# A 3x3 convolution with 2x2 max pooling on one core: a new program order, one half difference and four head operations on other engines

## The chip, the cores and the metric

The kernel runs on one core of a Trainium2 chip. The metric is the device time of one execution in microseconds (us). The core has five instruction queues, each worked through in order: PE (TensorE, matrix products, with its weight loads shown as PEld), DVE (VectorE), ACT (ScalarE), POOL (GpSimd) and SP (SyncE, which here only issues DMAs). They meet through semaphores alone.

## The reference

```python
x      = randn(16, 64, 64, 64)           # batch, c_in, h, w, float32
weight = randn(128, 64, 3, 3) * 0.1
x_pad  = pad(x, 1 on each side of h and w)
conv[b, co] += weight[co, ci, kh, kw] * x_pad[b, ci, kh:kh+64, kw:kw+64]   # over ci, kh, kw
output[b, c, i, j] = max(conv[b, c, 2*i:2*i+2, 2*j:2*j+2])                 # 16 x 128 x 32 x 32
```

## The kernel before, in words

Two images share the 128 partitions: lane h=0 is the first image of a pair (64 channels on partitions 0 to 63), h=1 the second. Each pair is cut into four bands of eight output rows (R = 8, so sixteen input rows), 32 *steps* s = 0 to 31 in all. For a step and a lane two PSUM banks of 8 x 64 are needed, `ta` and `tb`, out of eight.

The convolution of two neighbouring rows is not computed twice. By a row transform, differences and sums of the input rows meet differences and sums of the weight taps, so that two output rows cost four row products (five in K steps) instead of six. There are two kinds of steps:

- **K steps** (`KSTEPS`, ten) read bf16 rows straight from `kx`, which GpSimd's DMA queue loads with a cast to bf16 (LK, L109 and L114), and need only one sum of rows, KS (L356, VectorE). Their products are PA1, PA2, PB1, PB2 and PR.
- **W steps** (`WSTEPS`, twenty-two) read float32 rows from one of six buffers `wx`, loaded through SyncE (L and LB, L137; a buffer serves two steps). They need three transformed operands: E (`we`, L407: difference of neighbouring rows, GpSimd, or VectorE for the steps in `DIFF_ON_VECTOR`), D (`wd`, L416: difference over two rows, GpSimd, 128 x 1024) and WS (`ws`: sum of neighbouring rows, VectorE). WS has three forms: a two-operand addition (L395), a reduction (L387, steps in `SUM_BY_REDUCTION`), or, for `ODD_ROWS_IN_PSUM`, an addition whose second operand ScalarE has first copied to a PSUM bank (XC, L370, then L374). Their products are P2 (on E), P0 and P3 (on D) and P1 (on WS).

A *product* is three matmuls (L252), one for each column of the 3x3 kernel, on 64 rows of the array. Products of lane 0 and of lane 1 are issued in turn (`product`, L308), one matmul of each, so that both halves of the array work; two such products are called a pair here.

After the products: EV (L468 for K, L470 for W) copies `ta` to SBUF on ScalarE and frees its bank; SE (L481) copies `ta` to `tb` on ScalarE; MX (L498) takes the maximum of `tb` and EV's copy in place on VectorE, and later products (PR or P1), the same for both rows, are added on top; OD (L502) copies the odd columns out on ScalarE; CM (L508) takes the maximum over columns on VectorE and frees the bank of `tb`; ST (L516, L519) stores the step.

The *head* prepares the weights and the first two steps. The nine taps arrive in `wraw`. g0, g1 and g2 cast them to bf16 (L225 or L227); D2 and D0 are differences of taps (L539, L540); GS, GM and GP form sums (L541, L231, L233); u.. repeats a column (L182). T.. transposes a block on TensorE (L198) and V.. copies it to `wt` (L215 to L221). Step 0 has its rows cast in parts: XOa, XOb, XEa, XEb (L524 on ScalarE, L526 on VectorE), and step 2 by X1 and X2 (L533, ScalarE). F.k.part are the half products of step 0, G.k.part those of step 1; Ea and Eb (L428, VectorE) and Da and Db (`wd_half`, L436 to L449) are the half differences of step 1, and SEa, SEb its seeds (L494).

**What sets the order.** Nothing is reordered by a compiler. `ORDER` (L570) is one list of about 750 names; each engine gets its instructions in that order, and a name such as `MX.5.1` stands for step 5, lane 1. The list also decides which PSUM bank is taken (`free`, a queue). Two more waits are put in by hand: an operation of GpSimd made through `on_gpsimd` (L91) waits for the last operation made through `on_vector` (L87), that is the last VectorE operation on SBUF operands alone, reductions not counted; and a load named LB (`late_load`, L459) waits for the same. SyncE's queue holds loads and stores together.

Of the kernel before, what the change touches and what calls it, by code (L numbers as in the profile page):

```python
# [11 lines left out]
def kernel(  # L12
# [27 lines left out]
    SUM_BY_REDUCTION = (1, 3, 11, 12, 19, 20, 24, 25, 31,)  # L40
    ODD_ROWS_IN_PSUM = (4, 6, 8, 14, 17, 22, 23,)
    TURNED_BY_SCALAR = ("D0", "MP",)
    HALVES_ON_VECTOR = ()
    CAST_BY_SCALAR = ("XEa", "XOa", "XOb",)
    TAPS_BY_VECTOR = ()
# [119 lines left out]
    D2, G0, D0, G2, G1, GM, GP = BLOCKS.values()  # L165
# [401 lines left out]
    for m in PRODUCTS:  # L567
# [103 lines left out]
```

## Time and profile before

| | us |
|---|---|
| median of 3 runs | 104.76 (104.11 to 105.74) |
| the profiled execution | 104.74 |
| its span, first to last instruction | 102.9 |

The profiled execution's time exceeds its span by 1.8 us. In the lists of groups and in the timeline a row names the source line, the engine, the operation and its tiles (output <- input), and in brackets what ended the idle time before it. The granted clock of TensorE was full in every slice but the last. The largest loads on SyncE's queue are 480 to 576 KB each, and their median time from issue to landing is 9.0 us; from 2 to 27 us of the span the DMA engines are busy nearly throughout.

The groups of VectorE, ScalarE and GpSimd that carry most of the time besides the matmuls:

| line | what | count | mean ns |
|---|---|---|---|
| L416 POOL | D | 21 | 2361 |
| L407 POOL | E | 17 | 1273 |
| L498 DVE | MX | 64 | 689 |
| L508 DVE | CM | 64 | 414 |
| L387 DVE | WS by reduction | 9 | 1229 |
| L395 DVE | WS by addition | 6 | 764 |
| L470, L468 ACT | EV | 44, 20 | 611, 601 |
| L481 ACT | SE | 42 | 593 |

### The profile page before, as it was taken

Reading aid. Unit: us, or ns where it says so; the run is one execution under the profiler, and the core shown is the slowest. Engines: PE = TensorE matmul, PEld = TensorE weight load, DVE = VectorE, ACT = ScalarE, POOL = GpSimd, SP = SyncE. Lnnn points to the kernel's source line nnn. Section 1 sums busy time; section 2 is a strip of 40 time slices with the busy share of each in tenths; the row PEclk is TensorE's granted clock in tenths of the full one; section 3 lists DMA queues with packets and bytes.
Section 4 is the critical chain, followed back from the end, with each engine's and each line's share of the span. In section 5 each row is a group of like instructions: output and inputs, shape, how many; then the busy total and the mean of one; then the engine's idle time right before and its main releaser. Section 6 shows DMA issues by size and latency. Waiting matters only on the chain.

```text
span 102.9 us, 2528 instructions
## 1 busy us (share of the span) xinstructions
PE 96.5 (94%) x904; PEld 58.8 (57%) x904; DVE 90.0 (87%) x175; ACT 86.0 (84%) x192; POOL 79.8 (77%) x67
## 2 busy tenths in 40 slices
PE   6999999959999999999999999999999999999930
PEld 2475575525564556666666678877866655555400
DVE  1475999959998899999999999998999999799970
ACT  4569797579989799997898989899798899798740
POOL 6172998984995999979996999989599997981000
PEclk9999999999999999999999999999999999999996
DMA  2999999999839999999989868920881621159644
GB/s 68 321 345 305 261 344 344 358 423 314 158 83 295 317 270 362 283 344 411 421 324 130 147 206 197 324 84 0 241 253 47 232 80 38 64 181 322 218 156 151
DMA packets 13789, 24.25 MB, mean 236 GB/s; under 512 B 1104, under 2 KB 9296, under 8 KB 13776
## 3 DMA queue, kind: packets, MB, share of 16 engines
q1 hardware_dynamic: 12528, 21.73, 62.0%
q0 software_dynamic: 1104, 2.23, 13.4%
q8 instruction: 7, 0.11, 0.5%
q10 hardware_dynamic: 144, 0.13, 0.4%
q14 instruction: 6, 0.05, 0.2%
HBM read 17.92 MB, written 8.39 MB: 256 GB/s over the span
## 4 chain that ended last, share of the span: by engine, by line
PE 78%; DMA 10%; DVE 3%; ACT 3%; issue 1%; DVEq 0%; SPq 0%; ACTq 0%
PE acc L252 73%; DMA wx<-in_x_dram 10%; PE acc L628 3%; PE acc L198 2%; DVE o L508 1%; ACT ev L468 1%; ACT kx L533 1%; DVE acc L498 1%; ACT acc L370 1%; DVE ks L356 0%; DVE we L407 0%; DVE we L428 0%; DVEq L666 0%; SPq L137 0%; DVEq L498 0%
## 5 line engine op out<-in xcount | busy, mean ns | idle before, releaser
L252 PEld LDWEIGHTS <-wt 64*128 64x128 bf16 x870 | 55.8, 94 | 35.2 <-issue 3.3
L252 PE MATMUL acc<-wd,wt 64*128 64x504 bf16 (+3 forms) x276 | 53.9, 367 | 0.0
L416 POOL TENSOR_TENSOR wd<-wx 128x1024 bf16<-128x1024 f32 x21 | 49.3, 2361 | 3.3 <-DVE ks L356 3.1
L252 PE MATMUL acc<-kx,wt 64*128 64x504 bf16 (+6 forms) x264 | 45.0, 351 | 0.0
L498 DVE TENSOR_TENSOR acc<-acc,ev 128x512 f32<-128x512 f32 x64 | 42.0, 689 | 1.6 <-PE acc L252 1.1
L252 PE MATMUL acc<-we,wt 64*128 64x512 bf16 (+3 forms) x138 | 31.8, 367 | 1.3 <-ACT ev L468 1.2
L252 PE MATMUL acc<-ws,wt 64*128 64x512 bf16 (+1 forms) x132 | 32.5, 377 | 0.0
L470 ACT ACTIVATE ev<-acc 128x512 f32<-128x512 f32 x44 | 26.2, 611 | 2.1 <-PE acc L252 1.7
L481 ACT COPY acc<-acc 128x512 f32<-128x512 f32 x42 | 24.5, 593 | 1.9 <-PE acc L252 0.9
L508 DVE TENSOR_TENSOR o<-acc,od 128x256 f32<-128x256 f32 x64 | 24.9, 414 | 1.1 <-ACT od L502 0.9
L502 ACT COPY od<-acc 128x256 f32<-128x256 f32 x64 | 23.2, 384 | 2.5 <-PE acc L252 2.0
L407 POOL TENSOR_TENSOR we<-wx 128x512 bf16<-128x512 f32 x17 | 21.4, 1273 | 4.4 <-PE acc L252 3.8
L252 PE MATMUL acc<-ks,wt 64*128 64x504 bf16 (+1 forms) x60 | 13.6, 377 | 0.0
L468 ACT COPY ev<-acc 128x512 f32<-128x512 f32 x20 | 11.8, 601 | 1.9 <-PE acc L252 1.7
L387 DVE TENSOR_REDUCE ws<-wx 128x512 bf16<-128x1024 f32 x9 | 11.1, 1229 | 0.0
L374 DVE TENSOR_TENSOR ws<-wx,acc 128x512 bf16<-128x512 f32 x7 | 4.7, 677 | 1.5 <-ACT acc L370 1.5
L370 ACT COPY acc<-wx 128x512 f32<-128x512 f32 x7 | 4.2, 602 | 1.6 <-DMA wx<-in_x_dram 1.6
L356 DVE TENSOR_TENSOR ks<-kx 128x512 bf16<-128x512 bf16 x10 | 4.4, 449 | 0.6 <-ACT kx L533 0.6
L395 DVE TENSOR_TENSOR ws<-wx 128x512 bf16<-128x512 f32 x6 | 4.5, 764 | 0.0
L628 PE MATMUL acc<-const-bfloat16-1.0 128*128 128x512 bf16 x8 | 3.6, 625 | 0.8 <-PEq L652 0.8
L443 POOL TENSOR_TENSOR wd<-wx 128x512 bf16<-128x512 f32 x2 | 2.5, 1262 | 1.8 <-DVE we L428 1.8
L227 ACT CAST wq<-wraw 128x192 bf16<-128x192 f32 x3 | 1.5, 535 | 1.7 <-DMA wraw<-in_weight_dram 1.7
(33 smaller groups left out, 27.4 us busy)
## 6 DMA issues: line engine op xcount, KB each, us to landing
out_dram<-o SPq DMA_DIRECT2D x27, 256.0 KB, 3.7
wx<-in_x_dram SPq DMA_DIRECT2D x8, 512.0 KB, 9.4
wx<-in_x_dram SPq DMA_DIRECT2D x7, 576.0 KB, 8.3
wx<-in_x_dram SPq DMA_DIRECT2D x3, 544.0 KB, 10.2
kx<-in_x_dram POOLq DMA_DIRECT2D x3, 544.0 KB, 7.8
wx<-in_x_dram SPq DMA_DIRECT2D x3, 480.0 KB, 5.9
out_dram<-o SPq DMA_DIRECT2D x9, 128.0 KB, 4.4
ksecond<-in_x_dram SPq DMA_DIRECT2D x1, 544.0 KB, 5.1
```

The costliest lines, as they stand in the source:

```text
L252: nc.tensor.matmul(acc[t][:, i0:i1, o0:o1], wt[lo : lo + CI, tap_of(m0, kw, h), :], rows(lo, i0, i1, c0, c1), start=start and kw == 1, sto ...
L370: nc.scalar.copy(out=acc[copied[s]], in_=t[:, f + 1 : f + 2 * R : 2, :])
L387: nc.vector.tensor_reduce(out=row["ws", s], in_=t[:, f : f + 2 * R, :].rearrange("p (r two) w -> p r w two", two=2), axis=mybir.AxisListTy ...
L407: inst = (nc.vector if vector else nc.gpsimd).tensor_tensor(out=row["we", s], in0=t[:, f : f + 2 * R : 2, :], in1=t[:, f + 1 : f + 2 * R : ...
L416: nc.gpsimd.tensor_tensor(out=row["wd", s], in0=t[:, f + 1 : f + 1 + 2 * R, :], in1=t[:, f - 1 : f - 1 + 2 * R, :], op=SUB)
L468: nc.scalar.copy(out=ev[s, h], in_=acc[t])
L470: nc.scalar.mul(ev[s, h], acc[t], -1.0)
L481: nc.scalar.copy(out=acc[t], in_=acc[ta[s, h]])
L498: nc.vector.tensor_tensor(out=t, in0=t, in1=ev[s, h], op=MAX)
L502: nc.scalar.copy(out=od[s, h], in_=acc[tb[s, h]][:, :, 1::2])
L508: nc.vector.tensor_tensor(out=ot[s][:, h], in0=acc[t][:, :, 0::2], in1=od[s, h], op=MAX)
L628: nc.tensor.matmul(acc[n].rearrange("p a b -> p (a b)"), ones[:, 0:128], ones, start=True, stop=True, skip_group_check=True)
```

## The change

The list `ORDER` is replaced as a whole; six lists of names change with it. Step kinds, buffers, tiles and all functions stay.

```diff
-    SUM_BY_REDUCTION = (1, 3, 11, 12, 19, 20, 24, 25, 31,)
+    SUM_BY_REDUCTION = (1, 3, 11, 12, 19, 20, 24, 30,)
-    TURNED_BY_SCALAR = ("D0", "MP",)
-    HALVES_ON_VECTOR = ()
-    CAST_BY_SCALAR = ("XEa", "XOa", "XOb",)
-    TAPS_BY_VECTOR = ()
+    TURNED_BY_SCALAR = ("MP",)
+    HALVES_ON_VECTOR = ("Db",)
+    CAST_BY_SCALAR = ("XEa", "XEb", "XOb",)
+    TAPS_BY_VECTOR = ("g1",)
```

So Db goes from GpSimd to VectorE; g1, VD0 (the copy of transposed block D0) and XOa go from ScalarE to VectorE, and XEb from VectorE to ScalarE. Step 25 and step 31 get their sums by addition, step 30 by reduction. The start of the list, up to the place where both orders reach the products of step 4 and step 7:

```diff
-        g2 D2 g0 TD2 D0 TD0 XOa TG0 VD2 F.0.0 GS TG2 g1 XOb VG0 GM F.1.0 uG1 XEb LB.3 VD0 F.0.1 F.1.1 GP VG2 XEa
-        EV.0.1 L.11 X2 X1 LK.0.0 uGM F.2.0 PA1.2.0 KS.0 LB.4 Ea uGP F.3.0 TG1 KS.2 F.2.1 TMP Eb F.3.1 PA1.2.1
-        VMP LB.8 MX.0.1 EV.0.0 G.0.0 PA2.2.1 Da VG1 G.0.1 MX.0.0 SEa.0 SEa.1 Db LB.6 PA2.2.0 WS.1 SEb.1 PR.0.1
-        SEb.0 LK.0.1 E.3 PR.0.0 P2.3.1 PB1.2.1 EV.2.1 G.1.0 G.1.1 PB2.2.1 G.2.0 OD.0.0 G.2.1 EV.2.0 WS.3 EV.1.0
-        EV.1.1 PB1.2.0 PB2.2.0 CM.0.0 OD.0.1 SE.3.1 MX.1.0 CM.0.1 LB.9 D.3 MX.2.0 P2.3.0 P1.1.0 PR.2.0 P0.3.1
-        SE.3.0 P0.3.0 EV.3.1 MX.1.1 P3.3.1 P1.1.1 OD.2.0 MX.2.1 E.11 P3.3.0 MX.3.1 ST.0 PR.2.1 P1.3.1 OD.1.0
-        EV.3.0 PA1.5.0 PA1.5.1 E.4 OD.1.1 CM.2.0 CM.1.0 MX.3.0 CM.1.1 OD.2.1 PA2.5.1 PB1.5.0 P1.3.0 L.14 PB2.5.0
-        D.4 OD.3.1 XC.6 PA2.5.0 E.6 CM.2.1 L.12 P2.4.1 P2.4.0 CM.3.1 XC.4 PA1.7.0 LK.1.0 EV.5.1 PB1.5.1 WS.6
-        PB2.5.1 WS.4 L.16 SE.4.1 OD.3.0 PA2.7.0 P0.4.1 KS.5 P3.4.1 WS.9 KS.7 D.8 EV.5.0 SE.4.0 PA1.7.1 CM.3.0
...
+        g0 g1 g2 D2 XOb TG0 XEb uG1 TD2 TG1 TG2 D0 XOa LB.3 L.11 TD0 VD2 F.0.0 VG0 GS F.1.0 F.0.1 GM XEa VG2
+        F.1.1 EV.0.0 VD0 LB.4 EV.0.1 F.2.0 F.2.1 F.3.1 X1 LK.0.0 uGM KS.0 X2 GP uGP PA1.2.0 LB.6 VG1 F.3.0
+        MX.0.1 LB.8 TMP Ea KS.2 PR.0.1 VMP Eb OD.0.1 G.0.0 G.0.1 MX.0.0 SEa.0 PR.0.0 WS.1 Da Db SEa.1 E.3
+        PA1.2.1 SEb.1 PA2.2.0 LK.0.1 PA2.2.1 SEb.0 PB1.2.0 OD.0.0 G.2.0 CM.0.0 PB2.2.0 EV.2.0 WS.3 G.1.0 G.2.1
+        G.1.1 P2.3.1 EV.2.1 LB.9 L.14 D.3 PB1.2.1 EV.1.0 EV.1.1 SE.3.1 E.11 MX.1.0 PB2.2.1 CM.0.1 P2.3.0 P0.3.1
+        SE.3.0 P1.1.0 P3.3.1 EV.3.1 E.4 ST.0 MX.2.0 PR.2.0 P0.3.0 MX.1.1 P1.1.1 OD.2.0 P3.3.0 OD.1.0 MX.2.1
+        MX.3.1 PA1.5.0 PR.2.1 P1.3.1 CM.1.0 PA2.5.0 OD.1.1 CM.2.0 D.4 EV.3.0 XC.4 CM.1.1 MX.3.0 PB1.5.0 OD.3.1
+        PA1.5.1 WS.4 PA2.5.1 P1.3.0 CM.3.1 KS.5 L.17 EV.5.0 OD.2.1 PB2.5.0 E.6 P2.4.0 P2.4.1 XC.6 CM.2.1 WS.6
+        PB1.5.1 PA1.7.0 OD.3.0 SE.4.1 PB2.5.1 P0.4.1 CM.3.0 PA1.7.1 PA2.7.0 EV.5.1 SE.4.0 L.12 P0.4.0 KS.7 WS.9
...
```

GpSimd's queue in the middle, as the two lists give it (other engines' names left out):

```
before  D.3 E.11 E.4 D.4 E.6 LK.1.0 D.8 D.6 D.9 E.12 D.11 LK.1.1 D.12 E.14 D.14 E.19 E.16 D.16 D.15 E.17 E.20
after   D.3 E.11 E.4 D.4 E.6 LK.1.0 D.6 D.8 D.9 LK.1.1 D.11 D.12 E.12 E.14 D.14 E.19 E.20 E.16 D.15 D.16 E.17
```

SyncE's queue, loads and stores, from LB.3 on:

```
before  LB.3 L.11 LB.4 LB.8 LB.6 LB.9 ST.0 L.14 L.12 L.16 L.22 L.20 ST.2 ST.4 ST.5 L.19 L.15 ST.6 L.25 L.17 ST.1 L.24
after   LB.3 L.11 LB.4 LB.6 LB.8 LB.9 L.14 ST.0 L.17 L.12 ST.1 L.15 ST.2 L.16 L.22 L.19 ST.6 L.20 ST.3 L.25 ST.4 ST.7
```

## The prediction

> **What bounds the kernel now.** I read the page first, the share of each engine.
>
> ```profile
> ## 1 busy us (share of the span) xinstructions
> PE 96.5 (94%) x904; PEld 58.8 (57%) x904; DVE 90.0 (87%) x175; ACT 86.0 (84%) x192; POOL 79.8 (77%) x67
> ```
>
> TensorE has the largest share, but three others are within 17 points of it, so an average does not say which wait ends last. The chain of waits does. Its columns are start, length and what ran:
>
> ```profile
> 10.49 10.62 DMA wx<-in_x_dram
> ...
> 21.71 0.58 ACT acc L370
> 22.29 0.52 ACT ev L468
> ...
> 22.86 9.24 PE acc L252 x82
> ...
> 32.90 64.07 PE acc L252 x586
> ```
>
> Two things are to be seen. From 22.86 to 96.97 the chain is matmuls (L252), broken once, for 0.8 us: there only fewer or denser matmuls would shorten the run. Before that it is a load. I therefore asked the timeline what TensorE and ScalarE did around that load:
>
> ```profile
> 21.18 1.11 ACT L370 COPY acc<-wx 128x512 f32<-128x512 f32 x2 [1.59 <-DMA wx<-in_x_dram]
> ...
> 22.86 0.37 PE L252 MATMUL acc<-we,wt 64*128 64x512 bf16 x1 [1.16 <-ACT ev L468]
> ```
>
> ScalarE runs its queue in order. XC.6 (first of the two L370 copies) waits 1.59 us for the load LB.6, XC.4 and EV.5.1 (L468, over at 22.81 in the chain) stand behind it, and P2.4.0 on TensorE takes the PSUM bank that EV.5.1 frees. So TensorE stands for 1.16 us though it lacks no operand. I found no other hole of that size on TensorE between the first products and 97 us.
>
> How dense is the rest? The spacing of starts tells, since the busy share is modelled:
>
> ```profile
> 13.89 0.38 PE L252 MATMUL acc<-we,wt 64*128 64x512 bf16 x1
> ...
> 20.24 0.38 PE L252 MATMUL acc<-we,wt 64*128 64x512 bf16 x1
> ...
> 23.52 0.38 PE L252 MATMUL acc<-wd,wt 64*128 64x512 bf16 x1
> ...
> 32.43 0.38 PE L252 MATMUL acc<-wd,wt 64*128 64x504 bf16 x1
> 32.90 0.37 PE L252 MATMUL acc<-we,wt 64*128 64x512 bf16 x1
> ```
>
> The first two rows are the starts of P2.3.1 and P2.4.1, ten pairs of products apart: 6.35 us, 0.635 us a pair, 0.212 us for each of its three steps (I take 0.65 for pairs without the shorter 448-column products). The third is the start of P0.4.1, which I use below as a mark. The last two show a smaller hole: 0.47 us between two steps, 0.25 more than a step takes.
>
> **The change part by part.** The matmuls are the same, except for one zero seed (L491) that falls away, about 0.2 us, one step. The order on TensorE is nearly the old one too: the pairs of products from PB1.2.0 with P2.3.1 to the end are the same but for a few neighbours that swap. So the sum is made of waits.
>
> *The hole at 21.70.* SyncE now issues LB.6 ahead of LB.8, and ScalarE's queue reads XC.4, OD.3.1, EV.5.0, OD.2.1, XC.6, OD.3.0, SE.4.1, EV.5.1. Moreover P2.4.0 now takes the bank that CM.2.1 on VectorE frees. The two loads in the old order:
>
> ```profile
> L137 SPq DMA_DIRECT2D wx<-in_x_dram x2: 328/430/533, 10.1 to 10.5; - x2
> ...
> DMA to landing us min/median/max: 9.1/9.9/10.6
> ...
> 17.29 1.28 POOL L407 TENSOR_TENSOR we<-wx 128x512 bf16<-128x512 f32 x1 [0.31 <-DMA wx<-in_x_dram]
> ```
>
> LB.8 went at 10.1 and landed at 19.2, LB.6 at 10.5 and landed at 21.1; LB.4, for XC.4 and E.4, was there at 17.3. Swapped, LB.6 lands at about 19.2. XC.6 now stands behind EV.5.0, which reads the end of PA2.5.0, about 20.3, so ScalarE comes to it near 21.2, after the load. Even a landing at 21.1 would cost nothing there. The hole goes: minus 1.16 us. Next late is CM.2.1, done near 22.1 for a P2.4.0 due at 22.2; this is tight, and I keep 0.1 us for it.
>
> *Db on VectorE.* The price on the engines has near rows:
>
> ```profile
> 10.17 2.49 POOL L443 TENSOR_TENSOR wd<-wx 128x512 bf16<-128x512 f32 x2 [1.83 <-DVE we L428]
> ...
> 10.86 0.69 DVE L498 TENSOR_TENSOR acc<-acc,ev 128x512 f32<-128x512 f32 x1
> ...
> 11.46 1.23 DVE L387 TENSOR_REDUCE ws<-wx 128x512 bf16<-128x1024 f32 x1
> ...
> 12.60 0.68 DVE L407 TENSOR_TENSOR we<-wx 128x512 bf16<-128x512 f32 x1
> ...
> 13.38 2.36 POOL L416 TENSOR_TENSOR wd<-wx 128x1024 bf16<-128x1024 f32 x1 [0.18 <-DVE we L407]
> ...
> 15.79 0.37 PE L252 MATMUL acc<-wd,wt 64*128 64x512 bf16 x1
> ```
>
> GpSimd is spared half of 2.49 us; VectorE gets an operation of the shape of E.3 (12.60), 0.68 us, 0.60 from start to start. It stands between WS.1 and E.3. GpSimd's D.3 waits for E.3 (0.18 us in the row), and P0.3.1 (15.79) starts as D.3 ends, at 13.38 + 2.36 = 15.74. So the chain WS.1, Db, E.3, D.3, P0.3.1 has no slack, and what GpSimd saves does not reach it. The new VectorE queue is MX.0.1, Ea, KS.2, Eb, MX.0.0, WS.1, Db, E.3. MX.0.1 waits for F.3.0, which I put at 9.2 (below). By starts, 0.60 for a maximum, 0.34 each for Ea, KS.2 and Eb, 1.14 for the reduction, 0.60 for Db: WS.1 at 11.5 as before, E.3 at 13.2 and done at 13.9, D.3 from 13.95 to 16.3, P0.3.1 at 16.35. Cost: 0.56 us.
>
> Who else waits behind it? LB.9 on SyncE (behind E.3) goes 0.6 us later, at about 13.9; G.2.1 and G.1.1 need Db by 13.55 and have it at 13.3.
>
> *Head operations.* g1, VD0 and XOa go from ScalarE to VectorE, XEb the other way.
>
> ```profile
> 3.71 0.50 DVE L539 TENSOR_TENSOR wq<-wraw 128x192 bf16<-128x192 f32 x1 [2.58 <-DMA wraw<-in_weight_dram]
> ...
> 4.36 1.44 PE L198 MATMUL acc<-ident,wq 128*128 128x128 bf16 x12
> ...
> 6.17 0.28 DVE L526 CAST kx<-kfirst 128x256 bf16<-128x256 f32 x1
> ...
> 7.61 0.58 ACT L468 COPY ev<-acc 128x512 f32<-128x512 f32 x1 [0.94 <-PE acc L252]
> ...
> 8.10 1.19 ACT L533 CAST kx<-ksecond 128x512 bf16<-128x512 f32 x2
> ...
> 9.31 1.15 PE L252 MATMUL acc<-kx,wt 64*128 64x256 bf16 x12
> ...
> 9.41 0.81 ACT L215 ACTIVATE wt<-acc 128x768 bf16<-128x768 bf16 x1
> ...
> 10.29 0.82 PE L252 MATMUL acc<-we,wt 64*128 64x256 bf16 x12
> ```
>
> No row shows g1 cast on VectorE; its bounds are the cast of 256 columns (0.28) and the two-operand form on the same 192 columns (0.50). I take 0.3, the nearer kind. D2 is then done at 4.5 to 4.7 instead of 4.2. TensorE cannot use it before: its warm-up ends at 4.36 and TG0 (g0 on ScalarE, from 3.71) goes first now. Cost nothing, 0.2 if g1 takes the upper bound. The old head had TensorE at work from 4.36 to 10.29, where G.0.0 begins, and the new order gives it the same transposes and half products, so their end stays near 9.64 (9.31 and half of a row that holds one half product and a pair). What changes is the end: VMP now comes behind EV.0.0, EV.0.1, X1 and X2 on ScalarE, from about 7.7 (the old EV.0.1 went at 7.61, when F.1.1 was over): 1.0 for the two copies, 1.19 for the casts, 0.81 for VMP, so 10.7 against 10.22, and G.0.0 waits for it. Meanwhile PR.0.1, brought forward, fills 0.65 us. I find G.1.1 over at 14.2, against 13.89: 0.3 late. But P0.3.1 stands three pairs later, at 16.1, still ahead of D.3. The head's 0.3 lies inside the 0.56 and is not added.
>
> *Sums and the middle.* WS.25 and WS.31 become two-operand additions and WS.30 a reduction: minus 0.55 us of VectorE, late, beside matmuls that alone make the chain. Nothing. GpSimd's queue changes more: E.12 stood ahead of D.11 and now stands behind D.12.
>
> ```profile
> 24.45 7.00 POOL L416 TENSOR_TENSOR wd<-wx 128x1024 bf16<-128x1024 f32 x3 [1.32 <-DVE ks L356]
> ...
> 36.19 0.74 POOL L114 DMA_DIRECT2D kx<-in_x_dram  x1
> ```
>
> After: D.6 starts when WS.9 ends, about 24.1 (same queue of VectorE, 0.3 earlier). Three differences 7.0, LK.1.1 0.74, D.11 and D.12 4.67, E.12 1.28: done at 37.8. Its reader P2.12.1 is 23 pairs behind P0.4.1, due at 22.9 + 15.0 = 37.9. It fits by 0.1 us. I add 0.1 for such tight places.
>
> *A rule against the change.* GpSimd and VectorE can block each other:
>
> ```profile
> L395 DVE TENSOR_TENSOR ws<-wx x6: 676/680/1186, 23.3 to 93.3; 128x512 bf16<-128x512 f32 x6
> ...
> 50.69 2.51 POOL L407 TENSOR_TENSOR we<-wx 128x512 bf16<-128x512 f32 x2
> ...
> 52.56 1.79 DVE L395 TENSOR_TENSOR ws<-wx 128x512 bf16<-128x512 f32 x2
> ```
>
> One of six additions took 1186 ns instead of 680: it began at 52.56 while GpSimd worked until 53.20, and ended 0.54 us after that. The Trainium skill ("SBUF — State Buffer", section "SBUF: two separate sides") states that a VectorE operation with two SBUF inputs and a GpSimd operation exclude each other, whichever starts first holding the ports to its end; the trace agrees, with 1186 ns. For Db this means: Da starts when Eb ends (10.9) and runs 1.25 to 12.2, Db comes at 12.6, after MX.0.0 and WS.1. It clears Da by 0.4 us, so by this row too Db costs 0.60; were WS.1 not between them, it would cost about 0.7 more.
>
> *Sum.* Minus 1.16, plus 0.56, plus 0.1 for the bank of P2.4.0: minus 0.5. The other 0.1 and the zero seed's 0.2 I set against each other, and the hole at 32.65 I leave as it is (E.9 and CM.7.1 stand before P2.9.0 as they did). The tail after 96.97 has the same six maxima, copies and last stores. The profiled execution took 104.74 us around its span of 102.9, and the median is 104.76, so either base gives **104.2 us**.
>
> **The rivals.**
>
> *GpSimd becomes the bound; slower.* For it: E.12's margin of 0.1, the blocking, and LB.9 going later. Against it: 77% busy.
>
> ```profile
> DMA to landing us min/median/max: 4.1/9.0/11.4
> ```
>
> LB.9 took the median 9.0. From 13.9 that is 22.9, in time for WS.9. With the slowest landing, 11.4, WS.9 ends at 26.0, D.6 starts 1.9 late and P2.12.1 stands 1.8: minus 0.5 plus 1.8 makes **106.0**. It decides from the moment D.6 starts after 24.2. Each VectorE operation caught behind GpSimd (KS.13, KS.10, WS.15, WS.16 lie on that stretch) adds 0.5, so 107.5 with three.
>
> *All holes close; faster.* If VMP and Db find cover, the 0.56 falls away, and the 0.25 at 32.65 goes too: 104.74 − 1.16 − 0.25 = **103.3**. Against it: D.3 had 0.04 us of slack in the rows. For 2% even this is not enough.
>
> *The hole is filled but the time is not gained.* The head's debt doubles (VMP late, Db blocked) and D.17, GpSimd's next product without slack, sets the pace: 104.74 − 1.16 + 1.1 = **104.7**.
>
> **How the numbers follow.** Forecast 104.2 (103.6 to 104.6): 0.45. No gain, 104.7 (104.6 to 105.3): 0.15. GpSimd as the bound, 106.0 (105.3 to 107.5): 0.25, of which 0.14 lies above 106.9. All holes closed, 103.3 (102.4 to 103.6): 0.15, of which 0.05 is below 102.7 and 0.06 below 102.8. Leaving out these 0.06 at the bottom and 0.14 at the top, the range is 102.8 to 106.9. Two per cent, about what a measurement of this kernel can tell from no change, is 2.1 us: 102.7 and 106.9. Faster 0.05, same 0.81, slower 0.14.
>
> **What would show it.** Right, if TensorE has no idle before P2.4.0 near 22.2, XC.6's wait for its load is gone, D.3 starts near 13.9 behind Db and E.3, and P0.4.1 starts near 22.9 instead of 23.5. Wrong in the head, if the wait before P0.3.1 is over 0.3 us or G.0.0 starts after 11. Wrong in the middle, if TensorE waits for an E or D of GpSimd after 30 us, or L395, L407 or L356 on VectorE take well over 0.7 us. The chain's long stretch of matmuls, which ended at 96.97, would end near 96.5.

## The result, and the profile after

| | before | after |
|---|---|---|
| median of 21 runs each, us | 104.62 (103.91 to 107.07) | 104.12 (103.67 to 104.74) |
| ratio, 95% interval | | 0.9949 [0.9925, 0.9972] |
| profiled execution, us (span) | 104.74 (102.9) | 104.22 (102.5) |

The change saves half a microsecond, 0.5%: less than the 2% that counts as a difference here, but clear of zero. Shares first, part 1 of the page of the kernel after:

```profile
## 1 busy us (share of the span) xinstructions
PE 96.9 (95%) x903; PEld 62.7 (61%) x903; DVE 92.9 (91%) x178; ACT 85.8 (84%) x190; POOL 79.0 (77%) x66
```

One matmul fewer, the zero seed of the forecast. VectorE has gone from 90.0 to 92.9 us. Of these 2.9 us the groups further below put 1.7 down to waiting inside instructions; only the rest is work that the lists move to it. Next the chain of waits of the kernel after (start, length, what ran):

```profile
2.58 7.20 DMA wx<-in_x_dram
...
11.57 32.93 PE acc L252 x311
...
44.50 51.99 PE acc L252 x471
```

Matmuls carry it from 11.57 on; the load LB.6 and ScalarE's copies are gone from it. The last stretch ends at 44.50 + 51.99 = 96.49, against 96.97 before and 96.5 predicted. (A few last matmuls run beside the chain, up to 98.56 before and 98.10 after.) It looks like a sum that came out. To see whether the terms did, I set starts of the same products side by side:

| start of | before | after | difference | forecast |
|---|---|---|---|---|
| P2.3.1 | 13.89 | 14.25 | +0.36 | +0.3 |
| P0.3.1 | 15.79 | 16.38 | +0.59 | +0.56 |
| P2.4.0 | 22.86 | 22.05 | −0.81 | −0.66 |
| P0.4.1 | 23.52 | 22.78 | −0.74 | −0.6 |
| P2.9.0 | 32.90 | 31.80 | −1.10 | −0.5 from here on |
| P1.9.1 | 40.03 | 38.87 | −1.16 | |
| P1.14.0 | 46.47 | 45.60 | −0.87 | |
| P1.23.0 | 71.73 | 71.01 | −0.72 | |
| P1.24.0 | 83.24 | 82.74 | −0.50 | |
| end of the matmuls in the chain | 96.97 | 96.49 | −0.48 | −0.47 |

Read down the differences: +0.59 in the head, −1.40 at the hole, −0.35 more by 40 us, and then +0.68 given back in small steps. The forecast has the first two and the total; it has neither the third nor the fourth, and these nearly cancel. That they cancel is luck. The timeline of the kernel after, around head and hole:

```profile
9.81 0.43 DVE L428 TENSOR_TENSOR we<-wx 128x256 bf16<-128x256 f32 x1 [0.46 <-DMA wx<-in_x_dram]
...
12.58 0.68 DVE L443 TENSOR_TENSOR wd<-wx 128x512 bf16<-128x512 f32 x1
13.18 0.68 DVE L407 TENSOR_TENSOR we<-wx 128x512 bf16<-128x512 f32 x1
...
13.95 2.38 POOL L416 TENSOR_TENSOR wd<-wx 128x1024 bf16<-128x1024 f32 x1 [1.15 <-DVE we L407]
...
21.05 0.61 ACT L370 COPY acc<-wx 128x512 f32<-128x512 f32 x1
21.13 0.40 DVE L356 TENSOR_TENSOR ks<-kx 128x512 bf16<-128x512 bf16 x1
...
22.05 0.38 PE L252 MATMUL acc<-we,wt 64*128 64x512 bf16 x1
```

Ea (L428, first row) waits 0.46 us for its load. Db takes 0.68 us behind WS.1, E.3 follows 0.60 later, D.3 starts at 13.95 (forecast 13.95) and ends at 16.33, where P0.3.1 waits for it (16.38). XC.6 (L370) carries no wait for its load any more, and P2.4.0 starts at 22.05 with no pause ahead of it.

Where is the 0.68 given back? In slips between 39 and 42 us and in three small pauses of TensorE, at 44, 71 and 82, of 0.1 to 0.2 us each, where it stands for a maximum of VectorE that comes late. The largest two are P1.11.1 behind MX.11.1 and PR.26.0 behind MX.26.0, about 0.2 us each. The first, in the timelines of GpSimd, VectorE and TensorE of the kernel after:

```profile
42.02 1.27 POOL L407 TENSOR_TENSOR we<-wx 128x512 bf16<-128x512 f32 x1 [0.51 <-PE acc L252]
...
42.98 0.86 DVE L407 TENSOR_TENSOR we<-wx 128x512 bf16<-128x512 f32 x1
43.76 1.32 DVE L498 TENSOR_TENSOR acc<-acc,ev 128x512 f32<-128x512 f32 x2
...
44.12 0.38 PE L252 MATMUL acc<-wd,wt 64*128 64x512 bf16 x1
44.50 0.37 PE L252 MATMUL acc<-ws,wt 64*128 64x512 bf16 x1
```

E.15 (L407) takes 0.86 us where E.3, of the same shape, took 0.68: it began at 42.98 while GpSimd was in an E of its own until 43.29 (42.02 + 1.27), and ends 0.55 after that. MX.11.1 behind it starts at 43.76, and the two matmul starts at the end stand 0.38 apart, where a step takes 0.21. The same shows in the groups by line, first of the kernel after, then of before (busy us, mean ns of one):

```profile
L356 DVE TENSOR_TENSOR ks<-kx 128x512 bf16<-128x512 bf16 x10 | 5.7, 566 | 0.2 <-ACT kx L524 0.2
L395 DVE TENSOR_TENSOR ws<-wx 128x512 bf16<-128x512 f32 x7 | 5.5, 792 | 0.0
L407 DVE TENSOR_TENSOR we<-wx 128x512 bf16<-128x512 f32 x3 | 2.3, 779 | 0.0
```

```profile
L356 DVE TENSOR_TENSOR ks<-kx 128x512 bf16<-128x512 bf16 x10 | 4.4, 449 | 0.6 <-ACT kx L533 0.6
L395 DVE TENSOR_TENSOR ws<-wx 128x512 bf16<-128x512 f32 x6 | 4.5, 764 | 0.0
L407 DVE TENSOR_TENSOR we<-wx 128x512 bf16<-128x512 f32 x3 | 2.0, 682 | 0.0
```

Undisturbed, such an operation takes 0.41 us (L356) or 0.68 (the others). Above that, before lost 10 × 0.04 + 6 × 0.08 = 0.9 us, after 10 × 0.156 + 7 × 0.112 + 3 × 0.099 = 2.6 us. This is the blocking that the prediction quoted one row for; it has trebled. The reductions (L387, one input, 1.22 to 1.25) and the sums with one input in PSUM (L374, 0.67 to 0.69) show no such excess in either kernel.

### The profile page after: what moved, and what is told of

The parts are those of the page before. It is cut to its first block, busy times and chain, and to the rows that moved or that the text cites. A ratio compares the mean times of both kernels' runs of the same rounds, so it can differ in the third digit from the quotient of the medians.

```text
span 102.5 us, 2538 instructions
## 1 busy us (share of the span) xinstructions
PE 96.9 (95%) x903; PEld 62.7 (61%) x903; DVE 92.9 (91%) x178; ACT 85.8 (84%) x190; POOL 79.0 (77%) x66
## 4 chain that ended last, share of the span: by engine, by line
PE 83%; DMA 7%; DVE 4%; SPq 2%; issue 1%; DVEq 0%
PE acc L252 83%; DMA wx<-in_x_dram 7%; DVE o L508 1%; DVE acc L498 1%; DVE we L428 1%; SPq L151 0%; SPq L145 0%; SPq L144 0%; SPq L140 0%; DVE ks L356 0%; DVEq L666 0%
## 5 line engine op out<-in xcount | busy, mean ns | idle before, releaser
L252 PEld LDWEIGHTS <-wt 64*128 64x128 bf16 x870 | 59.8, 94 | 31.5 <-issue 4.4
L252 PE MATMUL acc<-kx,wt 64*128 64x504 bf16 (+6 forms) x264 | 43.8, 351 | 0.0
L407 POOL TENSOR_TENSOR we<-wx 128x512 bf16<-128x512 f32 x17 | 21.4, 1268 | 2.9 <-PE acc L252 1.7
L252 PE MATMUL acc<-ks,wt 64*128 64x504 bf16 (+1 forms) x60 | 14.3, 376 | 0.2
L387 DVE TENSOR_REDUCE ws<-wx 128x512 bf16<-128x1024 f32 x8 | 9.9, 1237 | 0.0
L356 DVE TENSOR_TENSOR ks<-kx 128x512 bf16<-128x512 bf16 x10 | 5.7, 566 | 0.2 <-ACT kx L524 0.2
L395 DVE TENSOR_TENSOR ws<-wx 128x512 bf16<-128x512 f32 x7 | 5.5, 792 | 0.0
L374 DVE TENSOR_TENSOR ws<-wx,acc 128x512 bf16<-128x512 f32 x7 | 4.7, 673 | 0.0
L370 ACT COPY acc<-wx 128x512 f32<-128x512 f32 x7 | 4.2, 603 | 0.1
L443 POOL TENSOR_TENSOR wd<-wx 128x512 bf16<-128x512 f32 x1 | 1.3, 1282 | 2.9 <-DVE we L428 2.9
L225 DVE CAST wq<-wraw 128x192 bf16<-128x192 f32 x1 | 0.5, 494 | 2.4 <-DMA wraw<-in_weight_dram 2.4
```

What stands on the lines that cost most here:

```text
L252: nc.tensor.matmul(acc[t][:, i0:i1, o0:o1], wt[lo : lo + CI, tap_of(m0, kw, h), :], rows(lo, i0, i1, c0, c1), start=start and kw == 1, sto ...
L356: nc.vector.tensor_tensor(out=row["ks", s], in0=t[:, f : f + 2 * R : 2, :], in1=t[:, f + 1 : f + 2 * R : 2, :], op=ADD)
L387: nc.vector.tensor_reduce(out=row["ws", s], in_=t[:, f : f + 2 * R, :].rearrange("p (r two) w -> p r w two", two=2), axis=mybir.AxisListTy ...
L395: nc.vector.tensor_tensor(out=row["ws", s], in0=t[:, f : f + 2 * R : 2, :], in1=t[:, f + 1 : f + 2 * R : 2, :], op=ADD)
L407: inst = (nc.vector if vector else nc.gpsimd).tensor_tensor(out=row["we", s], in0=t[:, f : f + 2 * R : 2, :], in1=t[:, f + 1 : f + 2 * R : ...
```

## The experiments

Twelve variants, of the kernel before where the name begins so or with "lb6", else of the kernel after. Ratios are to the kernel before, run on the same chip in the same job; the change itself has 0.9949 [0.9925, 0.9972]. The three lowest, before_lb6, lb6_db_vector and after_middle_old, cannot be told from one another or from the change.

| run | ratio [95%] | median us |
|---|---|---|
| before_lb6 | 0.9931 [0.9901, 0.9962] | 103.70 |
| before_xc6 | 1.0033 [0.9999, 1.0067] | 104.73 |
| after_lb8 | 0.9967 [0.9936, 0.9998] | 104.24 |
| after_db_gpsimd | 0.9996 [0.9963, 1.0029] | 104.34 |
| lb6_db_vector | 0.9935 [0.9902, 0.9968] | 103.80 |
| lb6_cm7 | 0.9999 [0.9967, 1.0030] | 104.39 |
| after_late_loads | 0.9984 [0.9953, 1.0016] | 104.27 |
| after_head_old | 1.0165 [1.0133, 1.0196] | 106.12 |
| after_middle_old | 0.9928 [0.9896, 0.9960] | 103.88 |
| after_relief | 0.9973 [0.9946, 1.0001] | 104.06 |
| after_ks5 | 0.9949 [0.9919, 0.9978] | 103.93 |
| after_sums_old | 1.0094 [1.0064, 1.0124] | 105.31 |

### The hole: the order of two loads, or the place of XC.6

**before_lb6.** The old order with only the two loads swapped on SyncE.

```diff
-VMP LB.8 MX.0.1
+VMP LB.6 MX.0.1
...
-Db LB.6 PA2.2.0
+Db LB.8 PA2.2.0
```

> The kernel before with one edit: LB.6 and LB.8 change places in SyncE's queue. Theory A (the whole pause of 1.16 us came from LB.6 landing at 21.1 under the waiting XC.6, and nothing else of the change was needed for it): LB.6 lands near 19.2, XC.6 starts near 19.6 with no wait, TensorE does not stand before P2.4.0, P0.4.1 starts near 22.3 instead of 23.52, the matmuls end near 95.8 instead of 96.97, and the time is 103.3 to 103.6, faster than the changed kernel's 104.1. Rival B (the pause is filled, but VectorE, busy 87 per cent and more after that, gives it back in later waits): P0.4.1 near 22.3 all the same, the matmuls end near 96.5, 104.0 to 104.4. Rival C (the load's place does not matter): 104.6, XC.6 still waits over 1 us.

Timeline of before_lb6, ScalarE and TensorE:

```profile
20.19 1.15 ACT L370 COPY acc<-wx 128x512 f32<-128x512 f32 x2
...
22.20 0.38 PE L252 MATMUL acc<-we,wt 64*128 64x512 bf16 x1
```

The two copies wait for nothing, where XC.6 waited 1.59 us. P2.4.0 comes at 22.20 instead of 22.86 although the head of this execution was 0.70 later than that of before. Counted from P0.3.1 that is a gain of 1.36 us, and nothing of it is given back: the matmuls in the chain end at 96.31 against 96.97, again 0.66 earlier. In the timed runs, one swap of two names gives as much as the whole replaced order, as far as the intervals tell. It fell a little short of the 103.3 to 103.6 expected; the timed runs leave no trace, so where the rest lies stays open.

**before_xc6.** The old order of loads, with XC.6 moved on ScalarE.

```diff
-D.4 OD.3.1 XC.6 PA2.5.0
+D.4 OD.3.1 PA2.5.0
...
-EV.5.1 PB1.5.1
+EV.5.1 XC.6 PB1.5.1
```

> The kernel before with one edit: XC.6 moves behind EV.5.1 in ScalarE's queue, and the loads stay as they are (LB.6 lands at 21.1). Theory A (the pause is EV.5.1 standing behind a waiting copy, so the order on ScalarE alone removes it): EV.5.1 is over near 20.8, P2.4.0 starts near 21.55, XC.6 starts near 21.1 to 21.3, time 103.3 to 103.7. Rival (the data of LB.6 are what is late: WS.6 and E.6 wait for the landing in any order and TensorE stands a little later): the pause moves to a reader of step 6 near 28, and the time stays at 104.3 to 104.6.

Timeline of before_xc6:

```profile
21.29 0.60 ACT L370 COPY acc<-wx 128x512 f32<-128x512 f32 x1
...
21.92 1.28 DVE L374 TENSOR_TENSOR ws<-wx,acc 128x512 bf16<-128x512 f32 x2 [1.29 <-ACT acc L370]
...
23.26 0.37 PE L252 MATMUL acc<-kx,wt 64*128 64x512 bf16 x1 [0.62 <-DVE ws L374]
```

P2.4.0 starts at 21.79, 1.07 earlier, and nothing is won. XC.6 fills the PSUM bank that WS.6 on VectorE adds up; VectorE now stands 1.29 us for it, and the next pair's product, PA1.7.0, 0.62 us for VectorE. P2.9.0 starts at 32.93, where it started in before (32.90); the head was 0.28 later. The load is still what all wait for; the wait has moved along three engines.

**after_lb8.** The new order with the old order of loads.

```diff
-PA1.2.0 LB.6 VG1
+PA1.2.0 LB.8 VG1
...
-MX.0.1 LB.8 TMP
+MX.0.1 LB.6 TMP
```

> The changed kernel with LB.8 ahead of LB.6 again on SyncE, nothing else. The prediction gave the filled pause to the swap of the loads first and to XC.6's later place second. Theory A (in the new order of ScalarE the place alone is enough: XC.6 stands behind XC.4, OD.3.1, EV.5.0 and OD.2.1 and is reached at 21.05, while LB.6 issued second lands at 20.0 to 21.0): XC.6 waits 0.2 us or less, P2.4.0 starts near 22.1, ratio 0.993 to 0.997 as for the change. Rival (the swap does the work here too): XC.6 waits 0.5 us or more, P2.4.0 or P0.4.1 starts 0.3 to 0.8 later, ratio 0.998 to 1.003.

LB.6 landed at 19.88, XC.6 did not wait, and P2.4.0 started at 22.18, 0.13 later than in the change, with a head 0.2 later. In the new order XC.6 comes so late on ScalarE that the swap of the loads is not needed. Either edit closes the hole in its own surroundings: in the old order the swap does and the move does not, in the new one the move alone suffices.

### Db on VectorE

**after_db_gpsimd.** The new order with Db on GpSimd again.

```diff
-    HALVES_ON_VECTOR = ("Db",)
+    HALVES_ON_VECTOR = ()
```

> The changed kernel with Db back on GpSimd and nothing else undone. By the prediction's step (Db on VectorE costs 0.56 us, since WS.1, Db, E.3, D.3, P0.3.1 have no slack), undoing it gives D.3 at 13.4, P0.3.1 near 15.8 and 103.6. Theory A, formed from the trace after (the head is late for another reason, a late load, and P2.3.1 stands at 14.25 whatever Db does; and E.3 on VectorE now finds GpSimd busy with Da and Db until 13.5, so it cannot end before 14.0): D.3 starts at 14.0 to 14.2, P0.3.1 at 16.4 to 16.6, time 104.0 to 104.4, no gain.

Timeline of after_db_gpsimd:

```profile
10.71 2.51 POOL L443 TENSOR_TENSOR wd<-wx 128x512 bf16<-128x512 f32 x2 [2.28 <-DVE we L428]
...
12.30 1.47 DVE L407 TENSOR_TENSOR we<-wx 128x512 bf16<-128x512 f32 x1
...
13.86 2.37 POOL L416 TENSOR_TENSOR wd<-wx 128x1024 bf16<-128x1024 f32 x1
```

E.3 takes Db's place at 12.30, finds GpSimd in Da and Db until 13.22 and takes 1.47 us instead of 0.68. D.3 starts at 13.86, 0.09 ahead of the version with Db on VectorE. The 0.56 that the prediction charged to Db is not had back by undoing Db: the blocking takes its place. From P0.3.1 to the end the products stay 0.1 us ahead of the change, as much as the head was; the two ratios cannot be told apart.

**lb6_db_vector.** before_lb6 with Db on VectorE, so that Db alone differs.

```diff
-    HALVES_ON_VECTOR = ()
+    HALVES_ON_VECTOR = ("Db",)
```

> The kernel before with LB.6 ahead of LB.8 (which alone gave 0.9931 of before) and, as the one further edit, Db on VectorE between WS.1 and E.3. The prediction's price for that was 0.56 us (WS.1, Db, E.3, D.3, P0.3.1 in a chain without slack): then E.3 and D.3 start 0.6 us later against WS.1 than in the run without it, P0.3.1 0.56 later, and the time is about 0.5 us above the single swap, ratio 0.997 to 0.999. Rival: the product before P0.3.1 is itself late, or GpSimd's Db held E.3 up just as long, so that the move costs 0 to 0.2 us: ratio 0.992 to 0.995.

The old list has Db ahead of WS.1, not between WS.1 and E.3 as the expectation has it. Db began at 11.48, 0.02 us after GpSimd's Da was over (10.19 + 1.27), and took 0.68. Timeline of lb6_db_vector:

```profile
16.40 0.37 PE L252 MATMUL acc<-wd,wt 64*128 64x512 bf16 x1
...
30.05 0.70 DVE L498 TENSOR_TENSOR acc<-acc,ev 128x512 f32<-128x512 f32 x1
...
31.73 0.37 PE L252 MATMUL acc<-we,wt 64*128 64x512 bf16 x1
```

The head of this execution equals that of before (P2.3.1 at 13.90), and P0.3.1 starts at 16.40, 0.61 later than before: the local price is what the prediction worked out. Yet the ratio stays, 0.9935 against 0.9931. About 0.4 of the 0.6 comes back at 31 us: P2.9.0 starts 9.65 us after P2.4.0, against 10.06 in before_lb6, where TensorE's starts stood 0.31 us apart at 31.02 and 0.48 at 31.78; here both pauses are gone. At the end of the matmuls in the chain (95.81) 0.2 is left, less than these ratios can tell. MX.6.0 (30.05) does not wait; in before_lb6 it stood idle for 0.46 us, to 30.58. The profile puts that wait down to TensorE, but P3.6.0 and EV.6.0, which MX.6.0 needs, were over by 30.07 there. What held it, and why it is not held here, stays open.

**lb6_cm7.** An attempt to remove these pauses directly: CM.7.1 earlier on VectorE.

```diff
-OD.7.1 MX.6.0
+OD.7.1 CM.7.1 MX.6.0
...
-P0.8.1 CM.7.1
+P0.8.1
```

> The kernel before with LB.6 ahead of LB.8, and CM.7.1 moved ahead of MX.6.0 on VectorE, into the 0.46 us that VectorE stands there at 30.1 (waiting for a product of step 6). Theory A (TensorE's small pause before P2.9.0 comes from VectorE: E.9 and the bank that CM.7.1 frees behind it): P2.9.0 has its bank early and starts as E.9 ends, the pause of 0.26 shrinks to 0.1 or less, matmuls after it come 0.2 to 0.3 earlier, ratio 0.989 to 0.992. Rival (E.9 itself is what ends last, or MX.6.0 made later holds P1.6.0): the pause stays or moves one pair up, ratio 0.992 to 0.995.

Timeline of lb6_cm7:

```profile
30.04 0.38 ACT L502 COPY od<-acc 128x256 f32<-128x256 f32 x1
30.45 0.42 DVE L508 TENSOR_TENSOR o<-acc,od 128x256 f32<-128x256 f32 x1 [0.85 <-ACT od L502]
30.79 0.69 DVE L498 TENSOR_TENSOR acc<-acc,ev 128x512 f32<-128x512 f32 x1
...
31.54 0.37 PE L252 MATMUL acc<-ws,wt 64*128 64x512 bf16 x1 [0.66 <-DVE acc L498]
```

A miss, slower than either expectation. CM.7.1 now stands in VectorE's queue ahead of its own operand, waits 0.85 us for ScalarE's copy, and MX.6.0 with TensorE behind it wait too. One place in one queue costs 0.7 us against before_lb6.

### The head

**after_late_loads.** The new order with three loads issued later.

```diff
-XOa LB.3 L.11 TD0
+XOa TD0
...
-VD0 LB.4 EV.0.1
+VD0 EV.0.1
...
-KS.0 X2 GP uGP
+KS.0 LB.3 L.11 X2 GP LB.4 uGP
```

> The changed kernel with LB.3, L.11 and LB.4 issued about 2 us later (LB.3 and L.11 behind KS.0, LB.4 behind GP), so not before 7.3 us where the change issues them at 5.15 to 6.0 and the kernel before at 6.5 to 7.6. Theory A (the three loads, issued earlier, take bandwidth from the first load of the head, whose landing went from 8.26 to 9.79, and Ea waits for it): the first part lands at 8.0 to 8.5, Ea starts at 9.35 behind MX.0.1 with no load wait, G.0.1 near 10.5 instead of 10.96, P2.3.1 near 13.8 instead of 14.25, D.3 near 13.5, time 103.6 to 103.8. Rival (the late landing is chance, or VMP and VectorE's queue set the head anyway): P2.3.1 stays at 14.2, time 104.0 to 104.3. A third way: LB.3 itself becomes late for E.3 (landing after 13.2), time 104.3 or more.

The first part of the first load landed at 8.77 instead of 9.79 and Ea did not wait for it, but P2.3.1 started at 14.42, no earlier than the 14.25 of the change. Its F.0.0 had begun at 6.50 (5.83 in the change), which the loads do not explain; see the last section. The earlier landing is not shown to be the edit's either: after_ks5, with these loads as in the change, had 8.79. No gain, and no support for the theory that the loads' sharing makes the head late.

**after_head_old.** The new order with g1, VD0, XOa and XEb on their old engines.

```diff
-    TURNED_BY_SCALAR = ("MP",)
+    TURNED_BY_SCALAR = ("D0", "MP",)
-    CAST_BY_SCALAR = ("XEa", "XEb", "XOb",)
-    TAPS_BY_VECTOR = ("g1",)
+    CAST_BY_SCALAR = ("XEa", "XOa", "XOb",)
+    TAPS_BY_VECTOR = ()
```

> The changed kernel with the four head operations on their old engines (g1, VD0 and XOa on ScalarE, XEb on VectorE) in the new order. Theory A (lateness of up to 0.6 us in the head is swallowed before 32 us, because there VectorE, not TensorE, sets the pace; but VD0 now stands behind EV.0.0 on ScalarE, so F.2.0 comes about 1.3 us later): P2.3.1 0.8 to 1.3 later, 0.4 to 0.8 of it left at P2.9.0, ratio 0.999 to 1.004. Rival (the head sets the end one to one): ratio 1.007 or more. Second rival (nothing arrives, since the head's order has cover): ratio 0.993 to 0.997.

Timeline of after_head_old:

```profile
10.65 0.59 ACT L217 COPY wt<-acc 128x512 bf16<-128x512 bf16 x1
...
11.30 0.94 PE L252 MATMUL acc<-kx,wt 64*128 64x256 bf16 x14 [1.16 <-ACT wt L217]
```

VD0 stands in ScalarE's queue behind EV.0.0, is copied at 10.65, and F.2.0 waits 1.16 us for it. The lateness is not swallowed: 106.12 against 104.12. (The profiled execution took 107.94; the page's row of the granted clock reads 7 and 5 tenths in its third and fourth slices, 5.3 to 10.6 us, and 9 in all slices after that, so the times of these rows are not those of the other runs, which lie at 105.75 to 106.30.) The four head operations, which the old order has on the opposite engines, are worth 2 us together in the new one. No run moves one alone; that VD0 is the one is read from this trace.

### The middle: operations that meet GpSimd

**after_middle_old.** The new order with the neighbourhood of E.12 as before: E.12 ahead of D.11, and LK.1.1, KS.13 and KS.10 behind D.11.

```diff
-MX.6.1 OD.7.0
+MX.6.1 E.12 OD.7.0
...
-P1.8.1 LK.1.1 EV.8.0
+P1.8.1 EV.8.0
...
-P0.9.1 WS.11
+P0.9.1 LK.1.1 KS.13 KS.10 WS.11
```

> The changed kernel with one stretch put back as it was: E.12 ahead of D.11 on GpSimd, LK.1.1 behind D.11, and KS.13 with KS.10 beside LK.1.1 instead of apart beside E.12 and D.14. Theory A (between 38 and 45 us the change gives back 0.3 us because VectorE is late: KS.13, KS.10 and E.15 began while GpSimd was computing and took 0.63, 0.48 and 0.87 us where 0.41, 0.41 and 0.68 are usual, and P1.11.1 waits for MX.11.1 behind them): the two sums are caught once at most, VectorE comes to MX.11.1 0.3 to 0.5 us earlier, the pause of 0.17 at 44.1 and the slips at 39 to 42 go, the matmuls end 0.2 to 0.3 earlier, ratio 0.991 to 0.993. Rival (the lateness shows up again at the next blocked operations, near 52 and 79, or D.12 made later holds P0.12.1): ratio 0.994 to 0.998.

Timeline of after_middle_old, VectorE and GpSimd:

```profile
34.98 0.79 DVE L356 TENSOR_TENSOR ks<-kx 128x512 bf16<-128x512 bf16 x2
35.10 0.74 POOL L114 DMA_DIRECT2D kx<-in_x_dram  x1
35.86 2.38 POOL L416 TENSOR_TENSOR wd<-wx 128x1024 bf16<-128x1024 f32 x1
```

The two KS run almost wholly while GpSimd issues a transfer instead of computing (D.11 ends at 35.14), and take 0.79 us together; in the change KS.13 alone took 0.63. The pause at 44 us is gone. At P0.3.1 (16.41) and P2.9.0 (31.81) this execution stands where the change does, and its matmuls in the chain end at 96.25, 0.24 earlier. Two pauses stay, at 71 (0.12) and at 82 (0.22). This is the lowest ratio of all, 0.9928, but its interval covers that of the change and of before_lb6.

**after_relief.** after_middle_old, with KS.21, KS.26 and KS.29 moved out of GpSimd's way as well.

```diff
-PB1.21.1 KS.26
+PB1.21.1 KS.21
...
-P1.20.0 KS.21
+P1.20.0
...
-WS.28 ST.19
+WS.28 KS.26 ST.19
...
-P0.25.0 KS.29
+P0.25.0
...
-MX.28.0
+MX.28.0 KS.29
```

> The changed kernel with five operations moved so that VectorE is caught behind GpSimd less: the middle as it was (E.12 ahead of D.11, LK.1.1, KS.13 and KS.10 together behind D.11), KS.21 in KS.26's place and KS.26 behind WS.28, KS.29 ten microseconds later. Theory A (what the change gives back after 39 us is VectorE's lateness, and it sits in pauses before P1.11.1 near 44, before P1.23.0 near 71 and before PR.26.0 near 82): on top of the middle's gain (ratio 0.9928) the pauses of 0.12 at 71 and 0.22 at 82 go, ratio 0.988 to 0.991, matmuls end near 96.1 to 96.4. Rival (VectorE has slack enough by 70, or the catches just move to the next operation): ratio 0.992 to 0.995.

Timeline of after_relief:

```profile
18.09 1.28 POOL L407 TENSOR_TENSOR we<-wx 128x512 bf16<-128x512 f32 x1 [0.98 <-DMA wx<-in_x_dram]
19.32 2.37 POOL L416 TENSOR_TENSOR wd<-wx 128x1024 bf16<-128x1024 f32 x1
...
20.68 1.29 DVE L356 TENSOR_TENSOR ks<-kx 128x512 bf16<-128x512 bf16 x1
...
22.36 0.37 PE L252 MATMUL acc<-we,wt 64*128 64x512 bf16 x1 [0.51 <-DVE o L508]
```

The pauses at 71 and 82 went, as expected, but in this execution LB.4 landed at 18.03 (16.57 in the change, 15.82 in after_middle_old), which the edit does not touch. E.4 and D.4 came later, KS.5 began at 20.68 inside D.4 and took 1.29 us instead of 0.40, and P2.4.0 paused for CM.2.1 behind it, the second wait that the prediction had named. In the change KS.5 starts at 21.13 and D.4 ends at 21.11 (18.76 + 2.35): 0.02 us of margin. The edit bought a second loss by itself: D.31 behind KS.29 was late, and WS.31 took 1.28 us.

**after_ks5.** after_middle_old with KS.21 and KS.26 as in after_relief, and KS.5 with E.6 taken out of D.4's reach.

```diff
-CM.3.1 KS.5 L.17
+CM.3.1 L.17
...
-PB2.5.0 E.6 P2.4.0
+PB2.5.0 P2.4.0
...
-CM.2.1 WS.6
+CM.2.1 KS.5 E.6 WS.6
```

> The changed kernel with the middle put back as before (E.12, LK.1.1, KS.13, KS.10), KS.21 in KS.26's place, KS.26 behind WS.28, and KS.5 (with E.6 behind it) placed behind CM.2.1 instead of ahead of it; KS.29 stays. Theory A (in the order of the change KS.5 begins 0.02 us after D.4 ends, and where the load LB.4 lands late, as in the run with five moved operations, it is caught for 0.9 us ahead of CM.2.1, whose bank P2.4.0 waits for): behind CM.2.1, KS.5 can no longer hold P2.4.0, and starts 0.3 us after D.4; TensorE has no pause over 0.2 us before P2.4.0, P1.11.1 and P1.23.0; ratio 0.989 to 0.992, the best of all. Rival (E.6 and what follows it on GpSimd, 0.35 us later, make WS.9 and D.6 late, or the late catch was a rare event): ratio 0.993 to 0.996, as the change or the single swap.

Timeline of after_ks5:

```profile
22.06 1.27 POOL L407 TENSOR_TENSOR we<-wx 128x512 bf16<-128x512 f32 x1 [0.91 <-DVE ks L356]
...
30.85 1.01 DVE L407 TENSOR_TENSOR we<-wx 128x512 bf16<-128x512 f32 x1
...
32.24 0.37 PE L252 MATMUL acc<-we,wt 64*128 64x512 bf16 x1
```

KS.5 is undisturbed and no pause stands before P2.4.0. But E.6, which waits for KS.5 on GpSimd, starts 0.45 later, D.9 behind it ends at 31.30, and E.9 on VectorE, begun inside D.9, takes 1.01 instead of 0.68; P2.9.0 follows at 32.24, 0.44 later than in the change. KS.7, begun inside E.6, takes 0.78. The ratio, 0.9949, is the rival's, and so is the cause, GpSimd late behind E.6: the catch has moved from 21 to 23 and 31 us. The pauses at 71 and 82 are gone here too.

### The sums

**after_sums_old.** The new order with the old list of reductions: steps 25 and 31 reduced, step 30 added.

```diff
-    SUM_BY_REDUCTION = (1, 3, 11, 12, 19, 20, 24, 30,)
+    SUM_BY_REDUCTION = (1, 3, 11, 12, 19, 20, 24, 25, 31,)
```

> The changed kernel with WS.25 and WS.31 as reductions again (WS.30 too). The prediction gave these edits nothing, because matmuls alone make the chain there. Theory A agrees for another reason: WS.25 as an addition was caught behind E.28 and took 1.21 us, as long as the reduction (1.23), so VectorE comes to MX.26.0 no later with the reduction; ratio 0.993 to 0.997. Rival (a reduction leaves VectorE later before PR.26.0 and in the tail, where WS.30 and WS.31 stand ahead of the last maxima): ratio 0.998 to 1.001.

Timeline of after_sums_old, and behind it the same place in the kernel after:

```profile
88.50 4.67 POOL L416 TENSOR_TENSOR wd<-wx 128x1024 bf16<-128x1024 f32 x2
...
91.36 2.36 DVE L395 TENSOR_TENSOR ws<-wx 128x512 bf16<-128x512 f32 x1
...
94.11 0.81 PE L252 MATMUL acc<-kx,wt 64*128 64x512 bf16 x6 [0.23 <-DVE o L508]
```

```profile
91.01 1.23 DVE L387 TENSOR_REDUCE ws<-wx 128x512 bf16<-128x1024 f32 x1
```

WS.30 as an addition begins at 91.36 inside D.31 (the second of the two differences in the first row, which end at 93.17) and ends 0.55 after it: 2.36 us for work of 0.68. As a reduction, also begun inside D.31, it takes 1.23. WS.31, now a reduction, adds 0.54 behind it (1.22 instead of 0.68). The maxima behind them on VectorE come late, and TensorE falls back: P2.31.0 (92.86) starts 0.35 us behind the change, PR.29.0 (97.07) 0.75. The run takes 105.31 against 104.12: the edit that the prediction booked at nothing is worth about 1.2 us in this order. The three sums were changed together; no run changes WS.30 alone.

## Why the prediction was right, and where only its sum was

**The hole: right.** Predicted −1.16 with 0.1 back. From P0.3.1 to P2.4.0 the profiles show −1.40, and before_lb6 and after_lb8 show that the order of the loads and XC.6's place are each enough, each in its own order. The term was read too small: 1.16 is the idle time behind the modelled end of the matmul at 21.32, which is drawn 0.38 long. By starts, as the prediction read the hole at 32.65, the pause is 1.54 less a step of 0.21, that is 1.33. The second wait that it expected, CM.2.1 for P2.4.0, was not seen in the change (CM.2.1 was done at 21.87).

**Db: right locally, in part by luck, and wrong in what it was worth.** +0.56 forecast, +0.59 measured at P0.3.1, +0.61 alone in lb6_db_vector, with a head equal to that of before. In the new order the +0.59 owes something to chance: the prediction had WS.1 at 11.5 because MX.0.1 would run at 9.2, but MX.0.1 ran at 8.65, and it was the late load under Ea that put WS.1 at 11.42. In after_relief, with the same queues there, WS.1 began at 10.98 and P0.3.1 at 15.94, 0.15 later than before, Db included. "If VMP and Db find cover, the 0.56 falls away" supposed that the time could be had. The runs that tried did not get it: undone in the new order E.3 is blocked instead, and done in the old order two thirds of the price come back at 31 us. The prediction applied the blocking rule to Db and did not ask what would stand in Db's place without it.

**The head: right in size by luck, wrong in the reason.** 0.3 late was forecast through VMP at 9.9 and G.0.0 at 10.75. VMP ran at 9.33 and G.0.0 began at 10.29; P2.3.1 was 0.36 late all the same, because Ea waited 0.46 us for a load that landed at 9.79 (8.26 before). That landing differs between executions: in after_relief it came at 9.35, and P2.3.1 started at 13.89, as in before. In the profiles of all variants but after_head_old, P2.3.1 lies between 13.89 and 14.6 with the old head as with the new, so one profile of each cannot show that the edit makes the head late. And g1, booked at 0.3 us, took 0.49, the upper bound; it cost nothing.

**The middle: two omissions that cancelled.** "The hole at 32.65 I leave as it is": it closed (−0.35 by 40 us), as it did in lb6_db_vector; why is not shown. "E.12's margin of 0.1" held: E.12 was done at 37.49 and P2.12.1 did not wait. But the step that gave VectorE's moved operations no price failed: KS.13, KS.10, E.15, KS.18, KS.26, KS.21, WS.28 and WS.25 were caught behind GpSimd, and 0.68 of the gain went. E.9 was caught too, by 0.1. The prediction had this mechanism only as an addition to a rival, named KS.13, KS.10, WS.15 and WS.16, and the last two were not caught; its own sign of being wrong in the middle, L395, L407 or L356 well over 0.7 us, did show. after_middle_old shows the cause at one place: without the catches of KS.13 and KS.10 the pause at 44 is gone. For the pauses at 71 and 82, after_relief and after_ks5 show the same with KS.21 and KS.26 moved. For the rest of the 0.68 the cause is argued from the trace alone, and no variant turned it into a time clearly below the change's.

**The sums: "Nothing" fits the sum, but for a reason that fails.** Against before, the difference of starts goes from −0.53 to −0.48 over the last 10 us of the matmuls. But the prediction counted duration (−0.55 us of VectorE) and not what runs beside it: with the old list the new order loses 1.2 us, and the addition WS.30, caught for 2.36 us, stands where the loss begins.

**The rivals.** The bound by GpSimd did not come: D.6 started at 23.86, ahead of the 24.2 from which it decides. That all holes close came near for a while: −1.16 at P1.9.1, of the −1.41 that this rival had. Then part of it was given back, as the third rival had it, but through VectorE and not through D.17, for which TensorE did not stand (P0.17.1, 56.74). So 104.2 was met by −1.40 + 0.59 − 0.35 + 0.68. The last two are nowhere in the forecast, and that they nearly cancel is luck.

## What to carry to other kernels

Where several engines are over 75% busy, cost a moved operation by what runs beside it at its new place, not by its duration alone: two-input operations of VectorE that begin while GpSimd computes paid the rest of GpSimd's operation and 0.3 to 0.55 us more here, and a slower form with one input can be the cheaper one. Before taking a new order as a whole, try the one edit that its largest wait asks for; here a swap of two loads gave as much as the whole new list, within what the runs can tell. When a forecast sum is met, check its terms on aligned starts, since a gain and a loss that were both overlooked can hide in it.

## What the runs showed of the hardware that was not expected

**A blocked operation can wait long.** The prediction knew 1.19 us for an addition of 0.68. KS.5 (0.40) took 1.29 in after_relief, E.3 1.47 in after_db_gpsimd and WS.30 2.36 in after_sums_old, each ending behind the GpSimd operation it had begun in. The Trainium skill ("SBUF — State Buffer", section "SBUF: two separate sides") says that the first holds the shared ports for the whole instruction and names VectorE operations with two SBUF inputs; the runs agree on both, with 2.36 us beside 1.23 us for the one-input form at the same place.

**The same transposes start alike and end 0.9 us apart.** The windows view, restricted to the transposes (L198), columns: stretch, its length, TensorE busy us and instructions running in it, the same for weight loads, granted clock, DMA share, GB/s; first the kernel after, then after_middle_old, whose first 8 us of queues are the same:

```profile
4.70:5.20 0.50, 0.50 (x8) 0.50 (x6) 1.00 1.01 377
5.20:5.70 0.50, 0.50 (x12) 0.50 (x9) 1.00 1.15 389
```

```profile
4.70:5.20 0.50, 0.50 (x8) 0.50 (x6) 1.00 1.23 226
5.20:5.70 0.50, 0.50 (x8) 0.50 (x6) 1.00 0.69 205
```

In the kernel after 8 transposes run in one half microsecond and 12 in the next; in after_middle_old 8 in both, and the 19 took 2.18 us instead of 1.67 (1.30 in after_relief). The column of the granted clock reads 1.00 in all four rows, but the clock records in the traces differ: full clock is recorded from 5.20 us in the kernel after, from 6.32 in after_middle_old and from 3.44 in after_relief. The transposes agree: in the kernel after their starts stand 0.107 us apart up to 5.15 and 0.056 from 5.24 on; in after_middle_old 0.107 throughout, in after_relief mostly 0.056. So these runs differ in when the full clock began. The Trainium skill ("TensorE: Matmul & The Clock Gate", section "Part 1: The HAM clock gate") has the matmul rate double at a moment that varies between runs of the same kernel; the rows fit this. With it F.0.0 moves from 5.68 (after_relief) to 6.34 (after_middle_old). A single profiled head is therefore uncertain by some 0.6 us, more than most terms argued about here.

**Loads land differently in unchanged queues.** The first part of Ea's load was there at 8.79 in after_ks5 and 10.14 in after_sums_old, and LB.4 at 15.82 in after_middle_old and 18.03 in after_relief; in both pairs the orders are the same beyond that point. With margins such as KS.5's 0.02 us, that alone decides whether an operation is caught.
